# Block 1's v rows in a PEER layer: three extra gather buffers used from the 73rd row on instead of from the first

## The chip, the cores and the metric

The kernel runs on one core of a Trainium2 chip. The metric is the device time of one execution in microseconds (us). The engines named below are PE (TensorE, the matrix multiplier), DVE (VectorE), ACT (ScalarE), POOL (GpSimd, which here issues the gathers) and SP (SyncE, which issues the plain loads and stores). All of them run their own instruction list in order and wait for each other by semaphores.

## The reference

One layer over 1024 tokens of width 1024: a hybrid of differential attention and a gated MLP, then a retrieval layer (PEER) over 16384 experts of one neuron each, then a norm. Only the retrieval layer matters here. It works on blocks of 128 tokens:

```python
    def block(xb):
        q = (xb @ w_q).reshape(PEER_TOKEN_BLOCK, PEER_HEADS, 2, PEER_HALF)
        s = jnp.einsum('thpd,hpnd->thpn', q, sub_keys).astype(jnp.float32)
        vals, idx = lax.top_k(s, K)
        cand = vals[:, :, 0, :, None] + vals[:, :, 1, None, :]
        best, flat = lax.top_k(cand.reshape(PEER_TOKEN_BLOCK, PEER_HEADS, K * K), K)
        ...
        expert = i1 * PEER_KEYS + i2
        g = jax.nn.softmax(best, axis=-1)
        h = jnp.einsum('thkd,td->thk', w_u[expert], xb)
        a = (g * jax.nn.gelu(h.astype(jnp.float32))).astype(xb.dtype)
        return jnp.einsum('thk,thkd->td', a, w_v[expert])
```

Each token picks 8 x 16 = 128 experts. For each it needs one row of w_u (a dot product with the token) and one row of w_v (added to the token's result with a weight).

## The kernel before

The eight blocks of 128 tokens are treated in two ways. Blocks 2 to 5 are **dense**: all 16384 experts are multiplied on PE, in 32 groups of four slices of 128 experts (function `dense`), and the weights of the experts that were not picked are zero. A slice needs 24 products into `hp` (L765 to L767), a gelu, the weights `gg`, and 24 products with w_v, of which six of eight output tiles stay in PSUM and two are added on DVE once a group (L791, tile `dacc`; two such additions a group, 64 in all). DVE also makes the low halves of the operands: `xl` once at the start (L727, eight pieces), and `ul`, `vl`, `ga`, `al` for each slice (L761, L779, L771, L775).

Blocks 0, 1, 6 and 7 are **gathered**: for each of a token's 128 experts, POOL issues one indirect DMA that fetches 128 rows of 1024 floats, one row for each token (`fetch`, L664), and DVE consumes it with one instruction: L685 for a row of w_u (tile `u`), L699 for a row of w_v (tile `v`, added into `y`). "Row j" below is such a fetch with its DVE step. There are 128 rows for u and 128 for v in each of the four blocks. A block's v ends with a norm and a store (L702 to L707).

In front of both stands the front part (function `front`): attention, gated MLP, the projections, the scores and their top-k on DVE (stage S, lines L565 to L569, tile `vi`), and the tables of weights for the dense blocks (`gates`: one-hot tiles `oh` by ACT and DVE L626, products `pgg` on PE L650, copied by ACT to `st` and stored to the scratch tensor `gd`). The second top-k and the expert numbers come from `select` (L163 to L226). For blocks 6 and 7 it runs after the front part; its three work tiles `sf`, `sb`, `so` then lie in the pool gat2. The front part's memory is given up where it ends, and two pools are opened on it: gat2 (three buffers) and those of `dense`.

The program is written as front, then "d u1 v0 v1 u6 v6 u7 v7" (L49, d is dense), but a scheduler puts the instructions of all engines into an order of its own from a simulated timeline, so that gathered rows stand between instructions of the front part and of the dense part. This order is fixed when the kernel is built.

A fetched row goes to one of five buffers of the pool gat, or to one of the three of gat2: `fetch` counts through eight places, and places 5 to 7 are in gat2 where the stage allows it. In the kernel before, the stages v1, u6, v6, u7 and v7 allow it:

```python
MIXED = "v1 u6 v6 u7 v7"
...
            if f"{src[2]}{b}" in MIXED and k_ >= GAT:
                t = gat2.tile([P, D], F32, name=f"{nm}", tag="gat2")
            else:
                t = gat.tile([P, D], F32, name=f"{nm}", tag="gat")
```

Of the kernel before, what the change touches and what calls it, by code (L numbers as in the profile page):

```python
# [27 lines left out]
NPAIR = PH * K  # L28
# [22 lines left out]
GAT = 5  # L51
# [1 line left out]
X4 = 2  # L53
UG = {3: 3, 4: 2}
WP = 3
MIXED = "v1 u6 v6 u7 v7"
OH2 = "d"
OH1 = "a"
TCK = dict(schedule_with_timeline_sim=True)
# [2 lines left out]
def peer_block(tc, d):  # L62
# [3 lines left out]
    with ExitStack() as ctx:  # L66
# [36 lines left out]
        def rsqrt(ms, n, inv, name, sm):  # L103

            v = sm.tile([P, 8], F32, name=name + "_v", tag="rs_v")[:, :n]
            y = sm.tile([P, 8], F32, name=name + "_y", tag="rs_y")[:, :n]
            t = sm.tile([P, 8], F32, name=name + "_t", tag="rs_t")[:, :n]
            dve.tensor_scalar(v, ms, inv, EPS, ALU.mult, ALU.add)
            dve.tensor_scalar(t.bitcast(I32), v.bitcast(I32), 1, None, ALU.logical_shift_right)
            dve.tensor_scalar(y.bitcast(I32), t.bitcast(I32), -1, 0x5F3759DF, ALU.mult, ALU.add)  # L110
            for _ in range(3):
                dve.scalar_tensor_tensor(t, y, -0.5, y, op0=ALU.mult, op1=ALU.mult)
                dve.tensor_tensor(t, t, v, ALU.mult)
                dve.scalar_tensor_tensor(y, t, 1.5, y, op0=ALU.add, op1=ALU.mult)
            return y
# [113 lines left out]
        def front():  # L229
# [350 lines left out]
            for w in PLAN.split():  # L580
                if w == "X":
                    wss.close()
                elif w == "Z":
                    att.close()
                elif w == "G1":
                    gates(G1B, vpsp, "vps", G1)
                elif w == "G2":
                    gates([b for b in DENSE if b not in G1B], smp, "smp", G2)
                elif w[0] in "uvt":
                    {"u": gather_u, "v": gather_v, "t": select}[w[0]](int(w[1:]))  # L590
                elif w[0] == "A":
                    stage_a(int(w[1]), w[3:])
                else:
                    steps[w[0]](int(w[1]))
# [59 lines left out]

        ring = [0]

        def fetch(b, src, ix, nm):
            k_ = ring[0] % (GAT + GAT2)
            ring[0] += 1
            if f"{src[2]}{b}" in MIXED and k_ >= GAT:  # L660
                t = gat2.tile([P, D], F32, name=f"{nm}", tag="gat2")
            else:
                t = gat.tile([P, D], F32, name=f"{nm}", tag="gat")
            pool.indirect_dma_start(out=t, out_offset=None, in_=d[src],  # L664
                                    in_offset=bass.IndirectOffsetOnAxis(ap=ix, axis=0))
            return t
# [3 lines left out]
        def gather_u(b):  # L670

            n = NPAIR
            ef, _, g = sel_t[b]
            idx = gxn.tile([P, n], I32, name=f"idx{b}", tag="idx", bufs=2)
            dve.tensor_copy(idx, ef)
            xn = gxn.tile([P, D], F32, name=f"xn{b}", tag="xn")
            x1 = gat.tile([P, D], F32, name=f"gx1{b}", tag="gat")
            pool.dma_start(x1, x1_d[b])
            gr = gat.tile([P, D], F32, name=f"gr{b}", tag="gat")
            pool.dma_start(gr, d["g_ffn_row"].partition_broadcast(P))  # L680
            dve.scalar_tensor_tensor(xn, x1, rs2_t[b], gr, op0=ALU.mult, op1=ALU.mult)
            h = gxn.tile([P, n], F32, name=f"h{b}", tag="h")
            for j in range(n):
                t = fetch(b, "w_u", idx[:, j:j + 1], f"u{b}_{j}")
                dve.tensor_tensor_reduce(t, t, xn, 1.0, 0.0, ALU.mult, ALU.add, h[:, j:j + 1])  # L685
            a = gxn.tile([P, n], F32, name=f"a{b}", tag="a")
            act.activation(a, h, AF.Gelu_apprx_tanh)
            dve.tensor_tensor(a, a, g, ALU.mult)
            G[b] = a, idx

        def gather_v(b):

            n = NPAIR
            a, idx = G[b]
            y = gxn.tile([P, D], F32, name=f"y{b}", tag="xn")
            pool.dma_start(y, x1_d[b])
            for j in range(n):
                t = fetch(b, "w_v", idx[:, j:j + 1], f"v{b}_{j}")
                dve.scalar_tensor_tensor(y, t, a[:, j:j + 1], y, op0=ALU.mult, op1=ALU.add)  # L699
            ms = smg.tile([P, 2], F32, name=f"msg_{b}", tag="msg")  # L700
            jk = gxn.tile([P, D], BF16, name=f"jk3_{b}", tag="jk", bufs=1)
            act.activation(jk, y, AF.Square, accum_out=ms[:, 0:1])  # L702
            r = rsqrt(ms[:, 0:1], 1, 1.0 / D, f"rl{b}", smg)
            gf = gat.tile([P, D], F32, name=f"gf{b}", tag="gat")
            pool.dma_start(gf, d["g_final"].partition_broadcast(P))
            dve.scalar_tensor_tensor(y, y, r, gf, op0=ALU.mult, op1=ALU.mult)
            sp.dma_start(d["out"][b * P:(b + 1) * P, :], y)  # L707
# [106 lines left out]
        for w in SEQ.split():  # L814
            if w == "d":
                dense()
            else:
                (gather_u if w[0] == "u" else gather_v)(int(w[1:]))
# [51 lines left out]
```

## Time and profile before

| What | us |
|---|---|
| median of 3 runs | 2804.43 |
| lowest and highest of them | 2799.83, 2818.26 |
| the profiled execution, whole | 2804.69 |
| its span, first to last instruction | 2802.8 |
| PE busy | 2457.4 |
| DVE busy | 2339.8 |
| POOL busy | 1506.5 |
| ACT busy | 1165.0 |

The span is 1.9 us shorter than the execution's own time. The front part ends at about 1291 us, the dense part's products run from about 1312 to 2732 us, and the gathered rows are spread from 275 us to the end.

### The profile page before, as it was taken

To read this page: it belongs to the slowest core of one execution; us is meant where nothing else is said; L and a number is where in the kernel's file an instruction comes from. 1 tells how busy PE (TensorE), PEld (TensorE's weight loads), DVE (VectorE), ACT (ScalarE), POOL (GpSimd) and SP (SyncE) were. 2 spreads that over 40 slices of the span, in tenths; PEclk is the share of its full clock that TensorE was granted. 3 is DMA by queue.
4 is the path that set the end of the run, shared out by engine and by line. 5 is a ranking of instruction groups with operands and counts; after the bars stand their busy time and mean duration, and the time that the engine had idled before them with its cause. 6 is when DMAs were issued, how large, how long until landed. Compare 5 with 4: busy or idle time off the path is not lost.

```text
span 2802.8 us, 33721 instructions
## 1 busy us (share of the span) xinstructions
PE 2457.4 (88%) x10764; PEld 1931.3 (69%) x10764; DVE 2339.8 (83%) x4967; ACT 1165.0 (42%) x2573; POOL 1506.5 (54%) x1139
## 2 busy tenths in 40 slices
PE   6789997996689767795999999999999999999990
PEld 5576654753457455684878878888888878888880
DVE  3449876999879999779998888888898788888898
ACT  4554332225863789896222323223232222323310
POOL 5262654447653346510666566565565577555665
PEclk9789998997789767795999999999999999999995
DMA  5155999998899679966999989999999999999998
GB/s 175 53 177 170 347 366 351 344 333 316 308 351 334 222 261 359 362 223 210 320 372 353 342 315 373 335 351 330 351 329 348 335 338 359 330 345 345 330 324 321
DMA packets 316513, 869.56 MB, mean 310 GB/s; under 512 B 26032, under 2 KB 93744, under 8 KB 312240
## 3 DMA queue, kind: packets, MB, share of 16 engines
q0 software_dynamic: 149760, 545.33, 53.1%
q1 hardware_dynamic: 166576, 322.09, 33.2%
q8 instruction: 84, 1.38, 0.2%
q14 instruction: 93, 0.76, 0.1%
HBM read 823.28 MB, written 44.04 MB: 309 GB/s over the span
## 4 chain that ended last, share of the span: by engine, by line
PE 40%; issue 16%; DVE 16%; POOL 11%; DMA 10%; ACT 6%; SPq 0%; POOLq 0%; DVEq 0%; ACTq 0%
POOL v L664 9%; PE pq L309 4%; PE hp L765 4%; PE hp L767 4%; PE hp L766 4%; DVE u L685 4%; PE y L744 3%; PE y L743 3%; PE y L745 3%; PE wo L309 3%; DVE y L699 3%; DMA v<-in_w_v_dram,idx 2%; DMA u<-in_w_u_dram,idx 2%; ACT oh L646 2%; PE wi L309 2%
## 5 line engine op out<-in xcount | busy, mean ns | idle before, releaser
L664 POOL DMA_INDIRECT v<-in_w_v_dram,idx x512 | 687.1, 1342 | 618.2 <-DVE y L699 326.9
L664 POOL DMA_INDIRECT u<-in_w_u_dram,idx x512 | 695.6, 1359 | 528.0 <-DVE h L685 235.2
L699 DVE SCALAR_TENSOR_TENSOR y<-v,a,y 128x1024 f32<-128x1024 f32 x512 | 656.2, 1282 | 36.8 <-DMA v<-in_w_v_dram,idx 24.8
L685 DVE CUSTOM_DVE_ANT_0 u<-u,xn 128x1024 f32<-128x1024 f32 x512 | 615.0, 1219 | 41.6 <-DMA u<-in_w_u_dram,idx 41.0
L765 PE MATMUL hp<-xh,uh 128*128 128x512 f32 x1024 | 402.6, 393 | 32.2 <-ACT uh L760 22.2
L767 PE MATMUL hp<-xh,ul 128*128 128x512 f32 x1024 | 400.8, 392 | 2.6 <-DVE ul L761 2.6
L766 PE MATMUL hp<-xl,uh 128*128 128x512 f32 x1024 | 401.3, 392 | 0.0
L778 ACT ACTIVATE vh<-vr 128x1024 fp32r<-128x1024 f32 x128 | 131.5, 1052 | 503.7 <-PE op L745 485.3
L650 PE MATMUL pgg<-oh,oh 128*128 128x128 f32 x1024 | 219.7, 368 | 114.3 <-ACT st L651 69.3
L743 PE MATMUL y<-vh,ah 128*128 128x512 f32 x768 | 298.8, 389 | 0.0
L744 PE MATMUL y<-vl,ah 128*128 128x512 f32 x768 | 298.8, 389 | 0.0
L650 PEld LDWEIGHTS pgg<-oh,oh 128*128 128x128 f32 x1024 | 186.9, 261 | 158.4 <-ACT st L651 81.9
L745 PE MATMUL y<-vh,al 128*128 128x512 f32 x768 | 286.1, 390 | 2.9 <-DVE al L775 2.9
L765 PEld LDWEIGHTS hp<-xh,uh 128*128 128x128 f32 x1024 | 194.2, 190 | 75.9 <-ACT uh L760 23.3
L646 ACT ACTIVATE oh<-oh,gT 128x128 f32<-128x128 f32 x512 | 221.9, 512 | 16.3 <-DVE gT L613 16.3
L767 PEld LDWEIGHTS hp<-xh,ul 128*128 128x128 f32 x1024 | 193.8, 189 | 44.0 <-DVE ul L761 3.3
L766 PEld LDWEIGHTS hp<-xl,uh 128*128 128x128 f32 x1024 | 194.1, 190 | 40.0
L760 ACT ACTIVATE uh<-ur 128x1024 fp32r<-128x1024 f32 x128 | 135.3, 1057 | 177.8 <-PE hp L766 165.5
L309 PE MATMUL pq<-sT,sc 128*128 128x256 f32 x768 | 186.0, 392 | 2.0 <-ACT sT L127 2.0
L761 DVE TENSOR_TENSOR ul<-ur,uh 128x1024 fp32r<-128x1024 f32 x128 | 156.3, 1221 | 19.9 <-ACT uh L760 19.9
L645 ACT ACTIVATE oh<-iota,gT 128x128 f32<-128x128 f32 x512 | 168.7, 420 | 7.7 <-PE pgg L650 7.6
L309 PEld LDWEIGHTS pq<-sT,sc 128*128 128x128 f32 x768 | 144.3, 195 | 34.6 <-issue 9.2
(439 smaller groups left out, 4141.3 us busy)
## 6 DMA issues: line engine op xcount, KB each, us to landing
ur<-in_w_uT_dram SPq DMA_DIRECT2D x128, 512.0 KB, 6.6
vr<-in_w_v_dram SPq DMA_DIRECT2D x128, 512.0 KB, 6.3
wi<-in_w_in_dram SPq DMA_DIRECT2D x80, 512.0 KB, 5.4
sc<-in_w_q_dram SPq DMA_DIRECT2D x64, 512.0 KB, 5.8
gd<-st SPq DMA_DIRECT2D x32, 1024.0 KB, 6.7
gg<-gd SPq DMA_DIRECT2D x16, 2048.0 KB, 22.2
wo<-in_w_out_dram SPq DMA_DIRECT2D x32, 512.0 KB, 7.0
x<-in_x_dram SPq DMA_DIRECT2D x16, 512.0 KB, 5.8
```

The source lines that it names most:

```text
L309: pe.matmul(ps, s_[i], m_[j], start=first and n == 0, stop=last and n == len(ops) - 1, **kw)
L646: act.activation(oh1[:, j, :], oh1[:, j, :], AF.Relu, scale=gT[:, 3, t_ + j:t_ + j + 1], bias=gT[:, 2, t_ + j:t_ + j + 1])
L650: pe.matmul(pg[:, j * P:(j + 1) * P], oh2[:, j, :], oh1[:, j, :], start=True, stop=True)
L664: pool.indirect_dma_start(out=t, out_offset=None, in_=d[src], in_offset=bass.IndirectOffsetOnAxis(ap=ix, axis=0))
L685: dve.tensor_tensor_reduce(t, t, xn, 1.0, 0.0, ALU.mult, ALU.add, h[:, j:j + 1])
L699: dve.scalar_tensor_tensor(y, t, a[:, j:j + 1], y, op0=ALU.mult, op1=ALU.add)
L743: pe.matmul(ps, ah[:, bs], vh[:, hs], start=first, stop=False, skip_group_check=True)
L744: pe.matmul(ps, ah[:, bs], vl[:, hs], start=False, stop=False, skip_group_check=True)
L745: pe.matmul(ps, al[:, bs], vh[:, hs], start=False, stop=last, skip_group_check=True)
L765: pe.matmul(hp[:, :TD], uh[:, ds_], xh[:, dc, :], start=(dc == 0), stop=False)
L766: pe.matmul(hp[:, :TD], uh[:, ds_], xl[:, dc, :], start=False, stop=False)
L767: pe.matmul(hp[:, :TD], ul[:, ds_], xh[:, dc, :], start=False, stop=(dc == DC - 1))
```

## The change

A stage now has a row number from which it uses the three late buffers, and v1 has 72. The other four stages keep 0, and the stages that had none have none. Rows 0 to 71 of v1 use the five buffers of gat at all eight places; since block 1's v begins at place 0, rows 77, 78 and 79 are the first in gat2. In the kernel before these were rows 5, 6 and 7. Nothing is added to or taken from the computation.

```diff
-MIXED = "v1 u6 v6 u7 v7"
+MIXED = {"v1": 72, "u6": 0, "v6": 0, "u7": 0, "v7": 0}
...
-        def fetch(b, src, ix, nm):
+        def fetch(b, src, ix, nm, j):
             k_ = ring[0] % (GAT + GAT2)
             ring[0] += 1
-            if f"{src[2]}{b}" in MIXED and k_ >= GAT:
+            if j >= MIXED.get(f"{src[2]}{b}", NPAIR) and k_ >= GAT:
                 t = gat2.tile([P, D], F32, name=f"{nm}", tag="gat2")
             else:
                 t = gat.tile([P, D], F32, name=f"{nm}", tag="gat")
...
-                t = fetch(b, "w_u", idx[:, j:j + 1], f"u{b}_{j}")
+                t = fetch(b, "w_u", idx[:, j:j + 1], f"u{b}_{j}", j)
...
-                t = fetch(b, "w_v", idx[:, j:j + 1], f"v{b}_{j}")
+                t = fetch(b, "w_v", idx[:, j:j + 1], f"v{b}_{j}", j)
```

The scheduler makes another order of it. On POOL, at the first rows of block 1's v (v_5 is row 5; the number behind it is a buffer's; + is the changed kernel, - the kernel before):

```order
 L664 DMA v_4_19185<-in_w_v_dram,idx_18367 128x1024
 L696 DMA y_19171<-x_1_87 128x1024
+L664 DMA v_5_19188<-in_w_v_dram,idx_18367 128x1024
+L664 DMA v_6_19191<-in_w_v_dram,idx_18367 128x1024
+L664 DMA v_7_19194<-in_w_v_dram,idx_18367 128x1024
 L664 DMA v_8_19197<-in_w_v_dram,idx_18367 128x1024
```

Rows 5 to 7 are issued in their turn; in the kernel before they stand behind row 12 and wait there for the front part's memory.

On DVE, where the first `xl` of the dense part stands, in the kernel before (`vi` and `rep` are the top-k of the front part, `sf` and `so` a late selection's work tiles):

```order
L214 TENSOR_TENSOR sf_10261<-so_10263 128x128
L176 MAX_INDEX sf_11430<-sf_11430 128x8
L179 MAX sf_11430<-sf_11430 128x8 x2
L176 MAX_INDEX sf_11430<-sf_11430 128x8 x2
L727 TENSOR_TENSOR xl<-xl,xh 128x512
L226 SCALAR_TENSOR_TENSOR ri_10327<-ri_10327,sf_10261 128x128
```

and in the changed one:

```order
L699 SCALAR_TENSOR_TENSOR y_19171<-v_40_19293,a_18760,y_19171 128x1024
L569 MAX_INDEX vi_8993<-vi_8993,rep_3_2_9402 128x8
L568 MAX vi_8993<-rep_3_3_9408 128x8
L699 SCALAR_TENSOR_TENSOR y_19171<-v_41_19296,a_18760,y_19171 128x1024
L569 MAX_INDEX vi_8993<-vi_8993,rep_3_3_9408 128x8
L727 TENSOR_TENSOR xl<-xl,xh 128x512
L163 TENSOR_TENSOR sf_10261<-vi_8992 128x8x16
```

Counted in the whole order, 42 rows of block 1's v (rows 0 to 41) stand ahead of the first `xl`, against 5 before, and the selection for block 6 begins behind it, where it was finished ahead of it before.

On DVE at the program's end, in the kernel before (block 7's v, and the dense part's last scaling, L808):

```order
L699 SCALAR_TENSOR_TENSOR y_20779<-v_108_21105,a_20776,y_20779 128x1024
L808 SCALAR_TENSOR_TENSOR last<-last,rl_y,gfin 128x1024 x3
L808 SCALAR_TENSOR_TENSOR dacc_9467<-dacc_9467,rl_y,gfin 128x1024
L699 SCALAR_TENSOR_TENSOR y_20779<-v_109_21108,a_20776,y_20779 128x1024
L699 SCALAR_TENSOR_TENSOR y_20779<-v_110_21111,a_20776,y_20779 128x1024
```

and in the changed one:

```order
L699 SCALAR_TENSOR_TENSOR y_20779<-v_127_21162,a_20776,y_20779 128x1024
L113 TENSOR_TENSOR rl_t<-rl_t,rl_v 128x4
L114 SCALAR_TENSOR_TENSOR rl_y<-rl_t,rl_y 128x4
L112 SCALAR_TENSOR_TENSOR rl_t<-rl_y 128x4
L113 TENSOR_TENSOR rl_t<-rl_t,rl_v 128x4
L114 SCALAR_TENSOR_TENSOR rl_y<-rl_t,rl_y 128x4
L808 SCALAR_TENSOR_TENSOR last<-last,rl_y,gfin 128x1024 x3
L808 SCALAR_TENSOR_TENSOR dacc_9467<-dacc_9467,rl_y,gfin 128x1024
```

Behind the dense part's last addition (L791) stand 15 rows of block 7's v, against 39 before, and all of them are ahead of L808; before, 19 of them stood behind it.

## Rows read from the trace of the kernel before

**Rows 1.** Busy time of each engine in two 70 us stretches: front part, dense part.

```profile
core 0: us, PE busy (x) PEld busy (x) DVE busy (x) ACT busy (x) POOL busy (x), PEclk, DMA share, GB/s
1120.00:1190.00 70.00, 55.83 (x231) 45.51 (x231) 52.32 (x51) 60.00 (x173) 41.55 (x36) 0.69 0.98 361
1470.00:1540.00 70.00, 70.00 (x311) 57.98 (x310) 60.90 (x59) 17.75 (x23) 44.60 (x32) 1.00 0.98 353
```

**Rows 2.** Waits of DVE from 1330 to 2735 us: total, times, longest.

```profile
DVE dacc L791 <- PE op L745: 135.4, 49, 7.2
```

**Rows 3.** DVE in order of time, tail: last addition to the last scaling.

```profile
2732.77 0.68 DVE L791 TENSOR_TENSOR dacc<-dacc,op 128x512 f32<-128x512 f32 x1
...
2748.31 0.16 DVE L108 TENSOR_SCALAR rl_v<-ms 128x4 f32<-128x4 f32 x1
...
2764.16 3.67 DVE L808 SCALAR_TENSOR_TENSOR last<-last,rl_y,gfin 128x1024 f32<-128x1024 f32 x3
2767.75 1.28 DVE L808 SCALAR_TENSOR_TENSOR dacc<-dacc,rl_y,gfin 128x1024 f32<-128x1024 f32 x1
2768.95 25.05 DVE L699 SCALAR_TENSOR_TENSOR y<-v,a,y 128x1024 f32<-128x1024 f32 x19
...
2797.53 1.28 DVE L706 SCALAR_TENSOR_TENSOR y<-y,rl_y,gf 128x1024 f32<-128x1024 f32 x1
```

**Rows 4.** POOL in order of time, block 1's first v rows.

```profile
1225.97 1.41 POOL L664 DMA_INDIRECT v<-in_w_v_dram,idx  x1 [0.30 <-issue]
1330.02 1.69 POOL L664 DMA_INDIRECT v<-in_w_v_dram,idx  x1 [102.63 <-ACT vh L778]
```

**Rows 5.** Busy time of each engine around the handover (columns as in Rows 1).

```profile
1205.00:1273.00 68.00, 62.35 (x350) 54.81 (x348) 49.96 (x224) 68.00 (x192) 8.98 (x7) 0.89 0.55 206
1205.00:1217.30 12.30, 12.30 (x71) 11.19 (x70) 4.12 (x9) 12.30 (x36) 1.71 (x2) 1.00 0.84 301
...
1273.00:1301.40 28.40, 13.09 (x45) 10.12 (x44) 27.89 (x138) 20.64 (x52) 0.00 (x0) 0.50 0.41 148
1301.40:1364.50 63.10, 48.97 (x197) 38.96 (x198) 59.12 (x114) 19.00 (x26) 21.33 (x17) 0.83 0.91 308
1364.50:1409.00 44.50, 44.50 (x198) 36.84 (x197) 41.25 (x41) 13.28 (x18) 28.47 (x21) 1.00 0.95 345
```

**Rows 6.** SP's queue at the end.

```profile
2798.84 0.33 SPq L707 DMA_DIRECT2D out_dram<-y  x1
```

**Rows 7.** DVE in order of time: front's end to the second `dacc` addition.

```profile
1205.36 1.27 DVE L706 SCALAR_TENSOR_TENSOR y<-y,rl_y,gf 128x1024 f32<-128x1024 f32 x1
...
1301.43 0.68 DVE L727 TENSOR_TENSOR xl<-xl,xh 128x512 fp32r<-128x512 f32 x1
...
1316.69 1.22 DVE L761 TENSOR_TENSOR ul<-ur,uh 128x1024 fp32r<-128x1024 f32 x1
...
1362.70 0.68 DVE L791 TENSOR_TENSOR dacc<-dacc,op 128x512 f32<-128x512 f32 x1
1363.30 1.28 DVE L699 SCALAR_TENSOR_TENSOR y<-v,a,y 128x1024 f32<-128x1024 f32 x1
1364.50 0.68 DVE L791 TENSOR_TENSOR dacc<-dacc,op 128x512 f32<-128x512 f32 x1
```

**Rows 8.** DMA issues from 1100 to 1190 us: count, KB, median us to landing.

```profile
sc<-in_w_q_dram SPq DMA_DIRECT2D x5, 512.0 KB, 12.0
v<-in_w_v_dram,idx POOLq DMA_INDIRECT x44, 7.6
```

**Rows 9.** PE in order of time, end of the front, start of dense.

```profile
1286.22 4.50 PE L650 MATMUL pgg<-oh,oh 128*128 128x128 f32 x16 [2.34 <-ACT oh L646]
1311.90 0.80 PE L765 MATMUL hp<-xh,uh 128*128 128x512 f32 x1 [21.18 <-ACT uh L760]
...
1317.96 0.80 PE L767 MATMUL hp<-xh,ul 128*128 128x512 f32 x1 [2.55 <-DVE ul L761]
```

**Rows 10.** ACT in order of time, just ahead of the first dense product.

```profile
1310.59 0.31 ACT L220 ACTIVATE g<-g 128x128 f32<-128x128 f32 x1 [7.32 <-DVE g L219]
```

**Rows 11.** DMA issues from 1190 to 1260 us (columns as in Rows 8).

```profile
sc<-in_w_q_dram SPq DMA_DIRECT2D x8, 512.0 KB, 4.9
```

## The prediction

> **What bounds the kernel now.** I read the busy times by stretch first. In the dense part PE is busy for 70.00 of 70 us at full clock, with 311 products [rows 1], and DVE, which works for 61 of them, loses its idle time to one thing: it waits 135.4 us in 49 pieces for PE's last product of a group [rows 2]. So from about 1320 to 2732 us PE sets the pace, and the gathered rows are fitted between the dense part's steps in a fixed order; what is not fitted in is left for the end. The end is bound by rows: PE has stopped, and DVE works off block 7's v. From the last `dacc` addition at 2732.8 us to the end of the span at 2802.8 are 70.0 us; 19 rows in one piece take 25.05 us, 1.32 us each [rows 3]. The time is therefore the start of the dense part, plus a nearly fixed dense length, plus a tail that depends on how many rows are left over.
>
> Ahead of the dense part is a hole that the change bears on. POOL issues row 12 of block 1's v at 1225.97 and its next one, row 5, at 1330.02 [rows 4]: 102.63 us without a gather, because row 5's buffer lies in memory that the front part still holds. The name given as releaser (an ACT copy of the dense part) is only the last of several semaphores; the order shows the row behind row 12 in its place. In this hole the DMA engines are busy for 0.55 and then 0.41 of the time, against 0.98 while gathers run [rows 1, 5].
>
> **The change, part by part.** It moves no work from one engine to another and adds no instruction, so the sum has two terms: the tail gets shorter, and the dense part starts later.
>
> *The tail.* By the order 15 rows are left behind the last addition instead of 39. Up to the L108 step (2732.77 to 2748.31, 15.5 us, with eight rows in it) nothing changes [rows 3]. Then seven rows at 1.32 are 9.3, four small steps at some 0.2 are 0.8, the four scalings take 4.8 (2764.16 to 2768.95), and block 7's norm, which can start at once because its last row is long done, some 2.5 up to the last scaling; that scaling and the issue of the store take 1.3 (2797.53 to 2798.84), and the store 4.0 to the span's end [rows 3, 6]. Sum 38.2 against 70.0: a gain of 31.8, which is also 24 rows times 1.32 = 31.7. This term hangs only on the fixed order and on durations that I see; the store may queue behind the four dense stores just ahead of it, which would cost 1 to 3 us. I take **-31.7**.
>
> *The start of the dense part.* Those 24 rows have to be done earlier, and DVE has to do them: 37 more rows ahead of the first `xl` (42 instead of 5). The step from one DVE instruction to the next behind a row is 1.20 us (1363.30 to 1364.50) [rows 7]. Between the end of block 0's v (1205.36) and the first `xl` (1301.43) DVE is busy for 49.96 of the first 68 us; the next 28.4 us are nearly all the selection for block 6, apart from some 3 us of one-hots and top-k [rows 5, 7]. That selection moves behind `xl`. So DVE now has 50.0 + 3.0 + 37 x 1.20 = 97.4 us of work in the piece, and cannot use the first waits of it (12.3 - 4.1 = 8.2 us until `y` has landed and row 0 can be added [rows 5]). 1205.4 + 105.6 = 1311.0, or 10 later than before. Can rows come so fast with five buffers? Between 1100 and 1190 us 44 rows were fetched in 90 us through the same five, 2.05 us each [rows 8]; 42 rows from 1217 on need 86 us and end at 1303, so the fetches just keep up, with some waits for single rows: I add 2. The gates and their stores are paced by ACT, which is busy for all 68 us of this piece [rows 5], and PE's last gate product ended at 1290.7 [rows 9], so 10 us of delay of the one-hots fit in before `xl` would wait for them.
>
> Behind the first `xl`, the chain to PE's start is: selection for block 6 up to its softmax, ACT's exponential, `uh`, `ul`. Before, ACT stood 7.32 us for the second selection's exponential [rows 10] and PE waited 21.18 us for `uh` and then for the first `ul` at 1316.69 [rows 7, 9]. Now the first selection is the one waited for, and the distance from `xl` to `ul` stays near 15 to 17 us. Up to the second addition DVE has 14 rows instead of 15 (-1.2) and the whole first selection (some 25 us [rows 5]) instead of the remaining part of the second: 59.12 busy, less 15 x 1.20 for rows and some 21 to 24 for the operands of four slices, leaves 17 to 20 for it. That is +4 to +7 net, and the piece had only 4 us of idle time (63.1 - 59.1) [rows 5]. Up to the fourth addition come 17 rows instead of 21 (-4.8), but most of the second selection, some 9 us, now stands there: +4, against 3.3 of idle time. What is lost here PE hardly gets back: a group is 192 products, 43.2 us at 70/311 each [rows 1], and it was 44.5 from the second to the fourth addition. With the 12 us ahead, 4 to 7 behind it, and a few us in which DVE now stands for the products of the first two slices, since PE begins late and, as before, below full clock (0.83 granted in the third stretch [rows 5]), I take **+20**.
>
> One wait is moved: the first rows in gat2 are now 77 to 79, which wait for the second selection's tiles; behind them POOL has rows 85 and on, and DVE's next step is row 77 itself. A fetch lands after 7.6 us in the middle [rows 8], of which the steps between hide a part; at most 7 us, once, while PE has products of two slices ahead. I count it at nothing, and at 7 if PE is hungry there.
>
> *Sum.* 2804.7 (profiled execution: span 2802.8 and 1.9 around it, 0.3 from the median) - 31.7 + 20 = **2793 us**, 0.4% below the median. Bounds of the second term: +8 if DVE alone counts and everything behind `xl` is absorbed by its idle time; +40 if the front part itself is slowed (below). A measurement of this kernel can hardly tell less than 1% (28 us) from nothing: the three runs lie 18 us apart.
>
> **The rivals.**
>
> *A crowded handover (slower).* The rows come back into a stretch in which the front part still loads w_q and stores the gates. With gathers running, an `sc` load landed after 12.0 us, and without them after 4.9 [rows 8, 11]: 7.1 more for each of eight loads, three of which can be under way, is 19 us of later scores, top-k and gates. The loads of `xl` and `gg` and the first `ur` then wait as well, some 5 more, and DVE's part behind `xl` adds its 11 (7 and the waits): +35, and the time is 2804.7 - 31.7 + 35 = 2808. It decides from a delay of 31.7 us on. Against it: in the stretch with 12.0 us the front part still went on, with ACT at 60 of 70 us [rows 1], and three loads ahead cover most of a landing.
>
> In the Trainium skill, "DMA: Bandwidth & Descriptors", section "Issuing engines are not separate DMA queues", says that transfers issued from SP and from GpSimd run on the same 16 engines and interleave. By that rule the 37 rows, 0.52 MB each at 355 to 361 GB/s, need 54 us of engines that idle for 47 us in the hole, so the front would be 7 us late by transfers alone; the landing times of 12.0 and 4.9 agree with it.
>
> *The dense part starts as before.* If DVE's idle time takes in all that is moved behind `xl`, the delay is the +8 to +10 ahead of it: 2781 to 2783. For it: DVE idles 18 us in the first piece. Against: 8.2 of these lie before the first row can be added, and behind `xl` there are only 7 us idle up to 1409.
>
> *It doesn't do what it says.* The hole moves to row 77 and POOL stands there as long as before. Then the rows done early are lost again in the dense part and the result is 2804. Against it: the order has the second selection finished with exactly 77 rows consumed, so there is nothing left to wait for but one landing.
>
> **How the numbers follow.** The forecast, a delay between 12 and 28 us, 2785 to 2801: 0.57. Dense part as before, 2776 to 2785: 0.17. Crowded handover, 2801 to 2815: 0.13; 0.04 of it and of unknown causes reach beyond 1% slower. The hole at row 77: 0.05. The last 0.08 is left for gains I don't see, such as PE's waits where a gathered block changes. The range 2779 to 2813 leaves out about 2 in 10. Faster by over 1% needs 2776, a delay under 4 us: 0.08. Slower by over 1% needs 2832: 0.04. Within 1%: 0.88.
>
> **What the profile after should show.** POOL: no wait over 20 us between 1200 and 1340, some 40 rows issued in it. DVE: first `xl` at 1309 to 1316, second addition at 1380 to 1390 (before 1364.5), last addition at 2745 to 2760, 15 rows behind it, and 38 to 41 us from there to the end. The `sc` landings between 1190 and 1260 rise from 4.9 us. I am wrong if the last addition comes before 2742 or after 2765, or if PE has new waits in the dense part behind 1480 us, since from there on the order gives DVE the same work as before.

## The result and the profile after

| | before | after |
|---|---|---|
| median of 6 runs each, us | 2806.54 | 2776.55 |
| lowest to highest | 2799.83 to 2818.26 | 2772.32 to 2785.89 |
| the profiled execution (its span) | 2804.69 (2802.8) | 2775.99 (2774.1) |

The ratio is 0.9895, with a 95% interval of 0.9877 to 0.9913: about 1% faster, 2.5 us beyond the fast end of the range that was given. The forecast of 2793 us is 17 us above the profiled execution.

The tail first. DVE in order of time in the changed kernel, from the last `dacc` addition to block 7's last scaling (start, duration, then engine, line and operation), and SP's queue at the end:

```profile
2736.79 0.69 DVE L791 TENSOR_TENSOR dacc<-dacc,op 128x512 f32<-128x512 f32 x1 [0.84 <-PE op L745]
...
2759.66 1.28 DVE L699 SCALAR_TENSOR_TENSOR y<-v,a,y 128x1024 f32<-128x1024 f32 x1
2761.84 3.68 DVE L808 SCALAR_TENSOR_TENSOR last<-last,rl_y,gfin 128x1024 f32<-128x1024 f32 x3
...
2768.93 1.28 DVE L706 SCALAR_TENSOR_TENSOR y<-y,rl_y,gf 128x1024 f32<-128x1024 f32 x1
```

```profile
2770.25 0.33 SPq L707 DMA_DIRECT2D out_dram<-y  x1
```

From the last addition to the end of the span are 37.3 us (38.2 forecast, 70.0 before [rows 3]). But that addition comes at 2736.8, only 4.0 us later than before, where +20 was forecast. The start of the dense part in order of time, on DVE, ACT and PE:

```profile
1201.43 1.27 DVE L706 SCALAR_TENSOR_TENSOR y<-y,rl_y,gf 128x1024 f32<-128x1024 f32 x1
...
1310.51 0.67 DVE L727 TENSOR_TENSOR xl<-xl,xh 128x512 fp32r<-128x512 f32 x1
...
1376.48 1.26 DVE L791 TENSOR_TENSOR dacc<-dacc,op 128x512 f32<-128x512 f32 x2
```

```profile
1325.75 0.31 ACT L220 ACTIVATE g<-g 128x128 f32<-128x128 f32 x1 [19.61 <-DVE g L219]
```

```profile
1327.06 0.80 PE L765 MATMUL hp<-xh,uh 128*128 128x512 f32 x1 [41.92 <-ACT uh L760]
```

The first `xl` moved from 1301.4 [rows 7] to 1310.5, as forecast, but block 0's last scaling (L706) had come 3.9 us earlier in this execution. The stretch ahead of it has nothing to do with the change, and it varies: in the 14 traces of this study that scaling lies between 1196.0 and 1212.6 us (1197.3 to 1212.6 in the five that are built on the kernel before, 1196.0 to 1210.4 in the nine built on the changed one; the means are 1204.8 and 1204.6). What lies just behind it repeats to 1.6 us where the order is the same: in the five traces built on the kernel before, the first `xl` is 96.0 to 97.2 us behind it and the second addition 159.1 to 160.7. So I compare distances from that scaling:

| us | before | after | difference |
|---|---|---|---|
| scaling of block 0, from the span's start | 1205.4 | 1201.4 | -3.9 |
| from it to the first `xl` | 96.1 | 109.1 | +13.0 |
| to the second addition | 159.1 | 175.6 | +16.5 |
| to the last addition | 1527.4 | 1535.4 | +8.0 |
| last addition to the end | 70.0 | 37.3 | -32.7 |
| scaling to the end | 1597.4 | 1572.6 | -24.8 |

The start does cost +16.5 (the forecast had 16 to 19 at this place). Between the second and the last addition, however, 8.5 us come back, where the forecast had a few more being lost and none coming back. The distances between pairs of `dacc` additions show where. They are 43.1 to 43.9 us in most groups, 43.5 on average. The exceptions lie in the first groups and where one gathered block changes to the next.

In the first groups the changed kernel does lose more, and more than forecast: the delay grows from 16.5 to 23.5 us (additions at 1629.3 before and 1648.8 after, each less its scaling). Then it shrinks twice. At the change from block 1 to 6 the kernel before takes 48.3 and 44.2 us for two groups; behind the first of them the delay is 18.6. At the change from block 6's v to block 7's u the distances are 50.4 and 46.6 us before (2243.9 to 2294.3 to 2340.9), and 43.7 and 43.5 after: the delay goes from 18.3 to 8.2, and it is 8.0 at the last addition. So 15.5 us come back, of which 7.0 had been lost behind the second addition.

These are single traces. How far the dense part repeats can be read where the order on DVE is the same: tail_alone (below) takes 1371.7 us from the second to the last addition, the kernel before 1368.3, and in three traces with the changed kernel's order the first two groups take 90.1, 90.9 and 98.4 us together. So a few us over the whole dense part, up to 9, can be chance. The stall at the change from block 6 to 7 repeats (97.0 and 96.2 us for two groups in the kernel before and in tail_alone), the one from block 1 to 6 less well (92.5 to 97.3 in four traces).

Busy times by group (columns as in Rows 1), the kernel before and then the changed one around the change from block 6 to 7:

```profile
2200.40:2243.90 43.50, 43.50 (x193) 36.03 (x192) 32.97 (x44) 13.76 (x19) 17.63 (x14) 1.00 0.85 308
2243.90:2294.30 50.40, 44.35 (x192) 35.39 (x190) 45.58 (x69) 14.84 (x18) 39.32 (x25) 0.99 0.89 325
2294.30:2340.90 46.60, 46.46 (x194) 38.34 (x195) 38.27 (x60) 10.95 (x15) 29.62 (x22) 0.94 0.99 380
```

```profile
2127.50:2171.00 43.50, 43.50 (x193) 36.02 (x193) 39.91 (x38) 12.63 (x16) 26.73 (x21) 1.00 0.97 346
2171.00:2214.70 43.70, 43.70 (x194) 36.18 (x194) 33.76 (x53) 13.69 (x19) 18.48 (x15) 1.00 0.90 311
2214.70:2258.20 43.50, 43.50 (x194) 36.02 (x193) 40.39 (x63) 12.38 (x17) 36.49 (x23) 1.00 1.00 378
```

Behind the window and its length, leaving out the counts, stand PE, PEld and then DVE. In the kernel before DVE has 33.0 us of work in one group and 45.6 in the next, more than the 43.5 that a group takes on PE; 12 gathered rows stand in the first and 25 in the second. In the changed kernel no group there has over 22 rows and 40.4 us. DVE of the kernel before in that overfull group, then waits (total, times, longest): PE's from 2243 to 2341 us, and DVE's for rows and POOL's longest from 2243.9 to 2294.3. The last line has the busy times right behind the group:

```profile
2232.79 1.29 DVE L706 SCALAR_TENSOR_TENSOR y<-y,rl_y,gf 128x1024 f32<-128x1024 f32 x1
2241.16 0.69 DVE L791 TENSOR_TENSOR dacc<-dacc,op 128x512 f32<-128x512 f32 x1 [7.08 <-PE op L745]
2243.88 0.69 DVE L791 TENSOR_TENSOR dacc<-dacc,op 128x512 f32<-128x512 f32 x1 [2.03 <-PE op L745]
...
2246.12 1.28 DVE L681 SCALAR_TENSOR_TENSOR xn<-gx,rs,gr 128x1024 f32<-128x1024 f32 x1
...
2292.56 1.23 DVE L685 CUSTOM_DVE_ANT_0 u<-u,xn 128x1024 f32<-128x1024 f32 x1 [2.08 <-DMA u<-in_w_u_dram,idx]
...
2293.71 1.28 DVE L791 TENSOR_TENSOR dacc<-dacc,op 128x512 f32<-128x512 f32 x2
```

```profile
PE hp L765 <- DVE dacc L791: 3.8, 1, 3.8
PE y L745 <- DVE al L775: 1.3, 2, 0.8
PE hp L765 <- ACT ga L770: 1.0, 1, 1.0
```

```profile
DVE u L685 <- DMA u<-in_w_u_dram,idx: 4.3, 5, 2.1
POOL u L664 <- DVE xn L681: 12.4, 1, 12.4
```

```profile
2294.30:2300.00 5.70, 5.56 (x14) 4.44 (x15) 5.28 (x8) 0.00 (x0) 4.49 (x4) 0.53 1.04 407
```

DVE stands idle for 9.1 us while nothing but the two additions is next in its order; then `xn` and 25 rows of u are due in one group, and at its end the additions come so late that PE waits for them. DVE's own work is 45.6 of the group's 50.4 us; most of the rest, 4.3 us, are waits for rows that have not landed. POOL could not fetch ahead: it stood for 12.4 us until `xn` was made and is then busy for most of the group (39.32 us, and 6.7 us between its issues). Both DVE's steps and POOL's fetches grow with the number of rows in the group, and the runs do not part them.

PE loses some 6 us of the 10 by waiting. Behind the waits its granted clock is 0.53 for 5.7 us, nearly all of them at 1.2 instead of 2.4 GHz, so the next group keeps PE busy for 46.46 us instead of 43.5: the other 3. In the changed kernel PE has no wait between 2171 and 2260 us, and the clock stays at 1.00.

The other signs: POOL's waits from 1200 to 1340 us have none over 16.1 us (102.6 before [rows 4]), and `sc` landings between 1190 and 1260 us rose from 4.9 [rows 11] to 6.0 only (waits, then DMA issues):

```profile
POOL v L664 <- DVE y L699: 25.7, 8, 9.9
POOL v L664 <- DVE y L706: 16.1, 1, 16.1
```

```profile
sc<-in_w_q_dram SPq DMA_DIRECT2D x8, 512.0 KB, 6.0
```

### The profile page after: what moved, and what is told of

It reads as the page before. It is cut to its first block, busy times and chain, and to the rows that moved or that the text cites. A ratio compares the mean times of both kernels' runs of the same rounds, so it can differ in the third digit from the quotient of the medians.

```text
span 2774.1 us, 33699 instructions
## 1 busy us (share of the span) xinstructions
PE 2442.2 (88%) x10764; PEld 1924.2 (69%) x10764; DVE 2333.6 (84%) x4967; ACT 1165.8 (42%) x2575; POOL 1509.2 (54%) x1139
## 4 chain that ended last, share of the span: by engine, by line
PE 56%; DVE 19%; DMA 9%; issue 8%; ACT 4%; POOL 3%; SPq 0%; POOLq 0%; DVEq 0%; ACTq 0%
PE hp L767 7%; PE hp L765 7%; PE hp L766 7%; PE y L743 5%; PE y L744 5%; PE y L745 5%; PE pq L309 3%; DVE u L685 3%; DMA v<-in_w_v_dram,idx 3%; DVE y L699 3%; PE wo L309 3%; POOL v L664 2%; PE wi L309 2%; PE op L744 2%; PE op L745 2%
## 5 line engine op out<-in xcount | busy, mean ns | idle before, releaser
L664 POOL DMA_INDIRECT v<-in_w_v_dram,idx x512 | 697.7, 1363 | 586.6 <-DVE y L699 326.6
L664 POOL DMA_INDIRECT u<-in_w_u_dram,idx x512 | 687.7, 1343 | 526.5 <-DVE h L685 235.3
L685 DVE CUSTOM_DVE_ANT_0 u<-u,xn 128x1024 f32<-128x1024 f32 x512 | 615.4, 1222 | 38.6 <-DMA u<-in_w_u_dram,idx 37.8
```

## The experiments

Three questions: is the tail worth its rows; what gives time back in the dense part; what holds up the start. Twelve kernels answer them. Their traces in distances from block 0's scaling, with the rows that the order leaves behind the last addition:

| kernel | first `xl` | 2nd addition | 2nd to last addition | tail | scaling to end | rows left |
|---|---|---|---|---|---|---|
| before | 96.1 | 159.1 | 1368.3 | 70.0 | 1597.4 | 39 |
| after | 109.1 | 175.6 | 1359.7 | 37.3 | 1572.6 | 15 |
| tail_alone | 96.1 | 159.4 | 1371.7 | 36.8 | 1567.9 | 15 |
| before_switch_mid_group | 97.2 | 160.7 | 1361.7 | 63.3 | 1585.7 | 35 |
| before_switch_group_end | 97.2 | 160.5 | 1375.4 | 40.1 | 1576.0 | 18 |
| after_switch_group_end | 110.5 | 175.8 | 1371.8 | 24.3 | 1571.8 | 4 |
| after_switch_mid_group | 109.3 | 176.2 | 1362.4 | 30.3 | 1568.9 | 10 |
| before_no_late_u | 96.0 | 159.4 | 1354.8 | 79.2 | 1593.5 | 47 |
| start_select_late | 110.0 | 169.2 | 1372.1 | 40.6 | 1581.9 | 18 |
| start_ur_first | 109.9 | 174.8 | 1362.5 | 37.7 | 1575.1 | 15 |
| start_both | 110.3 | 170.1 | 1369.0 | 40.4 | 1579.6 | 18 |
| v1_never_late | 109.0 | 176.4 | 1360.7 | 37.8 | 1574.9 | 15 |
| v1_late_from_24 | 101.3 | 165.9 | 1356.6 | 60.7 | 1583.1 | 33 |
| candidate | 110.7 | 186.3 | 1360.7 | 27.0 | 1574.0 | 7 |

### The tail alone

```diff
 # before
-            for j in range(n):
+            for j in range(n - (24 if b == 7 else 0)):
                 t = fetch(b, "w_v", ...
```

> The kernel before, with the last 24 rows of block 7's v left out (104 instead of 128, so this output block lacks them). Its order is that of the kernel before up to the last dacc addition; behind it 15 rows are left instead of 39. It prices the tail term by itself. The tail theory: last dacc addition at 2732.8 us as before, the rest 38 us instead of 70.0, whole 2773. Rival, that the tail has a floor of its own (the dense blocks' norm and four stores, with rows only beside them): a rest of 45 us or more, whole 2780 or more.

Measured: ratio 0.988 (0.985 to 0.991), 2775.64 us (2773 expected) against 2807.49 for the kernel before. The tail is 36.8 us, the second addition at 159.4 as before, and the change from block 6 to 7 takes 50.4 and 45.8 us again. So the tail theory holds, without a floor at 15 rows, and the overfull group is no accident of one execution.

### Is it the place of the block change in a group?

My first theory for what came back: what counts is where in a dense group the scheduler puts the change (`xn` right behind the additions, or between the operands of a group). Leaving out a few rows of block 6's v moves the change.

```diff
 # before with 8 or 20 fewer rows; after with 8 or 4
-            for j in range(n):
+            for j in range(n - (8 if b == 6 else 0)):
                 t = fetch(b, "w_v", ...
```

> The kernel before, with the last 8 rows of block 6's v left out (120 of 128, that block lacks them). By the order this moves the change from block 6's v to block 7's u: block 6 is scaled and the new xn made between the low halves of a group (behind the second and the third al of it), where the kernel before makes xn right behind a group's two dacc additions with the first u rows in one piece behind it. The start and the change from block 1 to 6 stay. Phase theory: the 50.4 and 46.6 us between dacc pairs there become 43.5 to 45, the last addition comes at 2722 to 2725 us instead of 2732.8; with four rows fewer behind it (35, -5 us), whole 2789 to 2792. Rival, a fixed dense length (what the changed kernel got back came from its fewer rows in the dense part, 569 against 581): here 577 rows stand there, at most 4 us earlier, whole 2796 to 2800.

> The kernel before, with the last 20 rows of block 6's v left out (108 of 128). A control: by the order the change from block 6's v to block 7's u lies at a group's end as in the kernel before, one group earlier, and 18 rows are left behind the last addition instead of 39. Phase theory: the 10 us at that change stay (two distances between dacc pairs that together are 95 to 98 us instead of 87), the last addition stays at 2730 to 2735, whole 2804.7 less 21 rows at 1.32 = 2777. If leaving rows out near the change were enough to remove its stall, the last addition would come at 2722 and the whole be 2767.

> The changed kernel, with the last 8 rows of block 6's v left out (120 of 128). By the order the change from block 6's v to block 7's u now lies at a group's end: block 6 is scaled ahead of the two dacc additions, xn and six u rows in one piece behind them, as in the kernel before. Phase theory: the changed kernel loses there the 7 to 10 us that it did not lose before, the last addition goes from 2736.8 to 2744 to 2747, with 4 rows behind it instead of 15 (-14 us); whole 2770. Rival, that the stall at the change hangs on the late buffers of v1 or on the later start and not on the place in the group: last addition at 2737, whole 2762.

> The changed kernel, with the last 4 rows of block 6's v left out (124 of 128). A control for the run with 8: the change from block 6's v to block 7's u stays at a group's beginning, between the first operands of it (block 6 scaled behind the dacc additions, xn behind the first al). Both theories: distances between dacc pairs there of 43.5 to 45 us, last addition at 2737, 10 rows behind it, whole 2776 less 5 rows at 1.32 = 2769.

Measured, in this order: ratio 0.9954 (0.9931 to 0.9977), 2789.95 us; 0.9907 (0.9876 to 0.9938), 2783.66; 0.9914 (0.9881 to 0.9946), 2781.1; 0.9892 (0.9851 to 0.9932), 2776.33. The first is as forecast; the other three lie 7 to 11 us above the whole times that the phase theory gave. The groups at and behind the change, one or two of each of the first three kernels:

```profile
2239.20:2283.50 44.30, 43.96 (x194) 36.06 (x194) 40.53 (x63) 12.62 (x17) 36.98 (x25) 1.00 1.01 381
```

```profile
2211.20:2259.50 48.30, 44.52 (x192) 35.34 (x190) 45.53 (x69) 14.43 (x18) 37.00 (x22) 1.00 0.84 307
2259.50:2311.00 51.50, 47.13 (x194) 38.37 (x195) 43.22 (x68) 11.29 (x16) 41.68 (x30) 0.93 1.00 370
```

```profile
2183.10:2229.30 46.20, 44.20 (x192) 35.41 (x190) 43.20 (x65) 13.21 (x17) 34.87 (x22) 1.00 0.89 326
```

With the change in mid-group the kernel before gets its two groups down to 43.5 and 44.3 us, as expected; with the change kept at a group's end it loses 12.8 us in two groups. The rival of a fixed dense length falls. But in the changed kernel with the change put to a group's end the loss is only 2.7 us, not 7 to 10, though `xn` stands right behind the additions. That group has 23 rows, not 25, and 43.2 us of DVE work, not 45.5. (The second to last additions are 12 us further apart in that run than in the changed kernel; 8 of it fell between 1380 and 1479 us, far from the change, in groups whose order on DVE is that of the changed kernel: this is the variation named above.) It takes 46.2 us although DVE's work alone would fit into 43.5: DVE also waits 2.5 us for rows there. The fourth kernel, the control, has 43.9 and 44.0 us at its change, as expected. The place alone is not the cause: the number of rows in the group fits better. The next run parts the two.

### Or the number of rows in the group?

Without late buffers for u, fewer rows are ready when `xn` comes. The order then has 16 and 15 rows in the two critical groups, at the same place, and nothing is left out.

```diff
 # before
-MIXED = "v1 u6 v6 u7 v7"
+MIXED = "v1 v6 v7"
```

> The kernel before, with u6 and u7 no longer using the three late buffers; nothing left out. Both block changes stay where they are, at a group's end (xn right behind the two dacc additions), but by the order only 16 and 15 rows stand in the first group behind them instead of 25 and 25. Theory, rows in a group: DVE's work there falls from 45.5 us to some 35, the distances between dacc pairs (48.3 and 44.2, 50.4 and 46.6) become 43.5 to 44.5, the last addition comes 13 to 16 us earlier than in the kernel before. Behind it stand 47 rows instead of 39, 8 x 1.32 = 11 us; whole 2800. Rival, the place in the group itself (xn late, PE's operands behind it): the distances stay, whole 2815.

Measured: 2800.74 us, ratio 0.9986 (0.9966 to 1.0007), with a last addition at 2714.6. The groups from block 1 to 6, and on both sides of the additions at the change from 6 to 7:

```profile
1624.10:1667.60 43.50, 43.50 (x193) 36.05 (x192) 35.10 (x51) 12.79 (x16) 25.56 (x18) 1.00 0.91 324
2189.90:2233.40 43.50, 43.50 (x194) 36.03 (x193) 36.73 (x47) 13.76 (x19) 19.48 (x17) 1.00 0.94 336
2233.40:2276.90 43.50, 43.50 (x193) 36.04 (x192) 34.08 (x50) 12.48 (x17) 23.20 (x17) 1.00 0.89 313
```

`xn` still stands right behind a group's additions (2236.74 behind 2233.37), and PE loses nothing: the second to last additions are 13.5 us closer than before. The rival of the place falls: it is the number of rows in the group that counts. Whether DVE's own work or the supply of rows weighs more in it stays open, since both went down here (in the group behind the second change POOL is busy for 23.20 us, against 39.32 in the kernel before). The gain does not reach the end, because the rows that do not fit are left over: 47 instead of 39, a tail of 79.2 instead of 70.0.

### What holds up the start?

In the changed kernel two things become ready within about 2 us of each other, close ahead of PE's first product (1327.06): ACT's exponential of block 6's selection (1325.75, `uh` is next) and the first `ur` (landed at 1323.7), which SP issues behind the 2 MB load `gg`.

```diff
 # after; start_select_late: LATE and v1 = 128 too; start_ur_first: only the second part; start_both: all
-LATE = {2: 6, 6: 7}
-MIXED = {"v1": 72, ...
+LATE = {0: 6, 3: 7}
+MIXED = {"v1": 128, ...
...
                 if gi in LATE:
+                    v_ = S["vi", LATE[gi]][0][:, 0, 0, 0:1]
+                    dve.scalar_tensor_tensor(v_, a_l.bitcast(F32)[:, 0:1], 0.0, v_, op0=ALU.mult, op1=ALU.add)
                     select(LATE[gi])
...
-                    sp.dma_start(gg, gd[:, :, gi * GRP:(gi + 2) * GRP, :])
+                    if gi:
+                        sp.dma_start(gg, gd[:, :, gi * GRP:(gi + 2) * GRP, :])
...
                     sp.dma_start(ur, d["w_uT"][e])
+                    if e == 0:
+                        sp.dma_start(gg, gd[:, :, 0:2 * GRP, :])
```

> The changed kernel with the two late selections held back until the first and the fourth dense group by a true dependency (a product with zero of a dense slice is added to their input), and with no late buffers for v1 at all, since the selections then hold them. So ACT's exponential of block 6's selection (1325.75 us in the changed kernel) no longer stands ahead of uh. Theory A, PE's start has two bounds at the same time, that exponential and the first ur (issued behind the 2 MB load gg on SP's queue, landed at 1323.7): PE's first product moves only from 1327.1 to about 1325, the second dacc addition from 1377.1 to about 1375. Rival, the exponential alone: first product at 1312 to 1316, second addition at 1364 to 1368. Three more rows stand behind the last addition (18), 4 us; whole 2778 by A, 2768 by the rival, both up to 10 more if the later block switch, which now ends at a group's end for v1 to u6, costs PE waits.

> The changed kernel with the first ur loaded ahead of the first gg on SP's queue, nothing else. Theory A (two bounds at the same time): the first ur lands near 1303 us, but uh still stands behind the exponential on ACT at about 1326, so PE's first product stays at 1326 to 1327, the second dacc addition at 1376 to 1377, whole 2775. Rival, that the load alone sets PE's start: first product at 1312 to 1316, whole 2765.

> The changed kernel with both edits of the two runs beside it: late selections held back, first ur ahead of gg. Theory A (two bounds): only here PE starts early, first product at 1312 to 1317 us (bound by the xl pieces, from 1310.5 on), second dacc addition near 1364 as in the kernel before, with 42 rows done ahead of the first xl. Whole: 2776 less 12 plus 4 for three more rows in the tail, 2768, if the selections' 50 us on DVE fit beside PE's dense work. Rival, that DVE's work up to the second addition sets the time (61.3 of 63 us busy there in the changed kernel): with the selection out of the way the addition comes early here but equally early in the run with the selections held back.

Measured: ratios 0.9925 (0.9900 to 0.9949), 0.9913 (0.9887 to 0.9940) and 0.9921 (0.9889 to 0.9952); 2787.02, 2783.79 and 2785.28 us. The first lies within theory A's 2778 and up to 10 more, the other two lie above what either theory gave. The second addition comes 6.4, 0.8 and 5.5 us earlier than in the changed kernel, by the distances above. Theory A (two bounds, 13 us for both edits together) falls: both edits bring no more than the first alone, as the last rival had it. Busy times from the first `xl`, or just ahead of it, to the second addition, of the changed kernel, of start_ur_first (with PE's longest wait for DVE there, below it) and of start_both (below it a wait of DVE from 1556 to 1612 us):

```profile
1310.50:1377.10 66.60, 47.59 (x192) 37.95 (x192) 65.33 (x191) 17.35 (x22) 24.07 (x15) 0.82 0.84 285
```

```profile
1319.00:1385.30 66.30, 49.53 (x192) 39.07 (x192) 66.20 (x191) 17.44 (x22) 23.03 (x16) 0.82 0.86 294
```

```profile
PE hp L770 <- DVE ul L764: 14.2, 2, 11.5
```

```profile
1313.30:1374.50 61.20, 49.15 (x197) 38.83 (x197) 48.99 (x85) 14.68 (x19) 28.11 (x18) 0.86 0.95 342
```

```profile
DVE xn L681 <- DMA out_dram<-y: 6.1, 1, 6.1
```

Where the selection stands in this piece, DVE is busy for all of it: with the first `ur` early, PE starts its first product 17 us earlier, where theory A had it stay, and then waits 11.5 us for DVE's `ul`. So in the changed kernel DVE's work sets the second addition, as the forecast had it. Only with the selection out of the way has DVE 12 us to spare. What then holds PE in start_both is not settled: it waits 8.6 us for DVE's `ul`, 2.2 for `xl` and 1.4 for `uh`, whose second `ur`, now behind `gg`, lands at 1330.6. What the later selections gain here they lose at the change from block 1 to 6 (a distance of 58.8 us in start_select_late, 53.9 in start_both). The last line is from there: `xn` waits 6.1 us until block 1's result is stored, since both use one buffer. That is a second way in which a block change stalls.

### The threshold, and a version of all three

```diff
 # after; thresholds 128 and 24 for v1 are the first two runs, the rest is the candidate
-MIXED = {"v1": 72, "u6": 0, ...
+MIXED = {"v1": 72, "u6": 128, ...
...
-                    sp.dma_start(gg, gd[:, :, gi * GRP:(gi + 2) * GRP, :])
+                    if gi:
+                        sp.dma_start(gg, gd[:, :, gi * GRP:(gi + 2) * GRP, :])
...
                     sp.dma_start(ur, d["w_uT"][e])
+                    if gi == 0:
+                        sp.dma_start(gg[:, :, k_, :], gd[:, :, k_, :])
+                        if k_ == 3:
+                            sp.dma_start(gg[:, :, 4:, :], gd[:, :, 4:8, :])
```

> The changed kernel with v1 never using the late buffers (threshold 128, the number of its rows, instead of 72). DVE's order is the same in every row as in the changed kernel. If only taking v1's first rows out of the late buffers matters, it runs as the changed kernel: last addition some 1535 us behind block 0's last scaling, rest 37 us, whole 2776. If the 18 or so late buffers' rows from row 77 on help the dense part, the distances between dacc pairs from 1423 to 1559 us grow by 2 to 10 us, whole 2778 to 2786.

> The changed kernel with the threshold 24 instead of 72. By the order 29 rows of v1 stand ahead of the first xl (5 before, 42 in the changed kernel), the selection for block 6 is ahead of it again, 33 rows are left at the end, and no group of the dense part has over 22 rows (the kernel before has 25 in two). Theory, start and rows in a group: first xl some 118 us behind block 0's last scaling (50 + 3 + 28.4 + 24 x 1.2 = 111 us of work and 8 of waits; before 96), second dacc addition some 181 behind it (before 159), both block changes at distances of 43.5 to 44.5 us, which gives back 15 of it, and 6 rows fewer in the tail 8: 2804.7 + 22 - 15 - 8 = 2804, as the kernel before. Rival, fixed dense length: 2819.

> The changed kernel with the first gg load cut in pieces (one slice of the table behind each of the first four ur, the second half behind the fourth), and u6 no longer using the late buffers. By the order 7 rows are left at the end instead of 15, 444 rows are done at the second dacc addition instead of 440, and 15 rows stand in the first group behind the change from block 1 to 6 with none over 21 behind it. Theory: 8 rows fewer in the tail, 10.6 us; 5 of the changed kernel's 6 us at its first block change come back; four rows more up to the second addition cost 4 to 5, since DVE has no idle time there (65.3 of 66.6 us busy): 2776 - 11 - 5 + 5 = 2765. Rival, that the cut load lets PE start so early that the first groups run short of DVE's operands, or that the tail is bound by the dense norm and its four stores from 7 rows down: 2772 to 2778, as the changed kernel.

Measured: v1_never_late 0.9927 (0.9903 to 0.9951), v1_late_from_24 0.9942 (0.9921 to 0.9963), candidate 0.9914 (0.9893 to 0.9935); 2783.96, 2788.31 and 2782.45 us.

Without any late buffer for v1 every distance in the table is within 2.3 us of the changed kernel's, and the interval overlaps its own. The order on DVE is not the same in every row, as had been expected: in the trace it parts from the changed kernel's behind 1443 us. The whole time lies in the range of the rival, that the late rows help; but the stretch that the rival had grow by 2 to 10 us, from the second to the fifth pair of additions, is 130.3 us long, against 135.9 in the changed kernel. So by the distances what works in the change is that v1's early rows no longer wait; that later rows use the three buffers is worth nothing that shows here.

With threshold 24 no group of the dense part has over 23 rows, and the second to last additions are 11.7 us closer than before, of 15 expected. The time is 2788, not 2804, since the start was mis-sized: the first `xl` comes 101.3 us behind the scaling, not 118, as only part of the selection stood ahead of it (its exponential at 1299.7, its end at 1327.7).

The candidate does not beat the changed kernel: its tail is 27.0 as expected, but the second addition comes 10.7 us later, of 4 to 5 expected. The first PE rows and the busy times from the first `xl` to that addition say why:

```profile
1304.62 0.79 PE L770 MATMUL hp<-xh,uh 128*128 128x512 f32 x1 [24.61 <-ACT uh L765]
1307.46 0.79 PE L771 MATMUL hp<-xl,uh 128*128 128x512 f32 x1 [2.04 <-DVE xl L727]
1319.80 0.80 PE L772 MATMUL hp<-xh,ul 128*128 128x512 f32 x1 [11.55 <-DVE ul L766]
```

```profile
1305.40:1382.30 76.90, 51.82 (x198) 40.49 (x198) 75.95 (x229) 20.24 (x24) 22.68 (x19) 0.78 0.93 276
```

DVE is busy for 75.95 of 76.90 us there. Eight rows fewer in the tail are bought with DVE's time at the start. Of the versions that leave no rows out, none was faster than the changed kernel.

## Why the prediction was wrong, point by point

- **The tail, -31.7.** Right: -32.7 in the changed kernel, -33.2 alone. The stores behind it cost nothing.
- **The start, +20.** Nearly right. First `xl` +13.0 (forecast 12), second addition +16.5 (16 to 19), fourth +18.3 (20). The reason given, that DVE's work sets it, is borne out: ahead of the first `xl` DVE is busy for 95.29 of 109.10 us (97.4 of 107.6 by the forecast's sum), behind it for 65.33 of 66.60, and start_ur_first shows PE waiting for it.

```profile
1201.40:1310.50 109.10, 72.57 (x393) 63.06 (x391) 95.29 (x260) 89.80 (x243) 44.78 (x43) 0.77 0.92 338
```

- **The step that failed: "a nearly fixed dense length", and "What is lost here PE hardly gets back".** The dense length was not fixed in the kernel before: in its trace the two block changes cost about 5 and 10 us beyond 43.5 a group, where 25 rows (45.5 us of DVE's work) stand in one group. The changed order has at most 22 rows there. The delay that the start had brought, 23.5 us ahead of the first of them, fell to 18.6 at the first and to 8.2 at the second. The forecast had looked at one stretch (1470 to 1540 us) and at one wait of DVE [rows 1, 2], and took the dense part for all alike; that wait, said to be all of DVE's idle time, is 135.4 of 193.5 us (1211.5 of 1405.0 busy from 1330 to 2735). It also said that behind 1480 us "the order gives DVE the same work as before", which is not so. The distances between additions (48.3, 50.4, 46.6 among 43.5) and the rows per group in both orders were there to be counted; "PE's waits where a gathered block changes" were named, at 0.08 with no price.
- **Where the 17 us between forecast and profile come from.** 8.5 less in the dense part than at its start, 3.5 of start, 1.0 of tail and 3.9 from block 0's scaling coming early in this one execution, which is no effect of the change.
- **The crowded handover.** It falls where it was put: `sc` landings 6.0 us, not 12.0, and the front's gate products ended at 1285.1, before at 1290.7 [rows 9]; that is 83.7 and 85.4 us behind the scaling. The loads do crowd behind it: the two loads of `gg` there landed after 22.8 us in the middle instead of 13.2. This agrees with the Trainium skill, "DMA: Bandwidth & Descriptors", section "Issuing engines are not separate DMA queues", by which DMAs that different engines issue run on the same 16 DMA engines and interleave. DVE is late there anyway; what the crowded loads would cost by themselves no run shows.
- **The dense part starts as before.** The measured delay of the last addition, 8.0 us, is this rival's +8, but by luck: the start was late by 16.5 us and more, and most of that was given back up to 900 us on.
- **It doesn't do what it says.** It does: no POOL wait over 16.1 us.
- **The wait of row 77**, counted at nothing, was nothing: v1_never_late has no such wait and the same distances.
- **Signs of being wrong.** "If the last addition comes before 2742" was met (2736.8). So was "new waits in the dense part behind 1480 us": PE waits 2.0 us for a `dacc` addition at 1559; the kernel before has no such wait from 1480 up to its first block change at 1629.

Open: the changed kernel has one distance of 47.1 us (1512.1 to 1559.2) with 21 rows and 41.2 us of DVE work, and the candidate one with 21 and 40.9. In the first, DVE waits 5.6 us for one `vh` of ACT; in the second, at its change from block 6 to 7, 3.0 us for rows and 2.8 for a `uh`. This was seen only, not tested. So under 43.5 us of work in a group is not enough when DVE also waits in it.

## What to carry to other kernels

A stage that is bound by one engine "throughout" is to be checked group by group: list the distances between its periodic steps, and where one stands out, count what the in-order helper engine has to do in that group and what it waits for. When a scheduler makes a new order, count the same in the new one; a change at one end can fill or empty a group far away. A wait removed ahead of such a stage is worth the rows that it takes out of the tail, less what they cost the engine that feeds the stage's start.

## What the runs showed of the hardware

- The same instruction order repeats to 1.6 us over 160 us behind a common step (five traces), while that step itself lies between 1196.0 and 1212.6 us in 14 traces. Distances from a step that both kernels share show a few us there that whole times, which spread over 10 us and more, do not. Further on they need repeats too: two groups of one order took 90.1 to 98.4 us in three traces.
- A wait of PE was followed by a stretch at the lower granted clock: about 6 us of waits in two groups, then 0.53 over 5.7 us, which cost some 3 us more.
- A load issued right behind a large one on SP's queue can be held up while it is issued, not only while it lands: behind the 2 MB of `gg` the issue of the first `ur` took 9.26 us in the kernel before and 21.86 in the changed one (both below), ahead of `gg` 0.42 (start_ur_first).

```profile
1297.07 9.26 SPq L757 DMA_DIRECT2D ur<-in_w_uT_dram  x1
1294.30 21.86 SPq L757 DMA_DIRECT2D ur<-in_w_uT_dram  x1
```
